# GpSimd's weight splits in feed-forward blocks go to VectorE, and modulation products get windows of steps

## The chip, the core and the metric

One core of a Trainium2 chip runs the whole program. Its engines are TensorE (PE, with PEld for its weight loads), VectorE (DVE), ScalarE (ACT), GpSimd (POOL) and SyncE (SP, whose queue issues most transfers). The metric is device time in microseconds: the median of several runs. Beside it stands one execution that the hardware profiler recorded; durations are read from that one.

## The reference

Two transformer blocks for 256 tokens of width 1024, in fp32. The parts run one after the other, each on what the one before has left in `x`:

```python
x = x + mamba2_mixer(x, ...)                 # first block, layer 0
x = x + conv_ffn(x, ...)                     # ffn0
x = x + diff_attention(x, ...)               # layer 1
x = x + conv_ffn(x, ...)                     # ffn1
mod = silu(c) @ w_ada + b_ada                # 6 x 1024, needed by the second block only
sh1, sc1, ga1, sh2, sc2, ga2 = split(mod, 6)
x = x + ga1 * mixer(rms_norm(x, g_mix) * (1 + sc1) + sh1)   # dsa: attention and a recurrence
x = x + ga2 * conv_ffn_2(rms_norm(x, g_ffn) * (1 + sc2) + sh2)   # ffn2
return rms_norm(x, g_final)

def conv_ffn(x, ln_g, up_w, conv_w, conv_b, down_w):
    u = causal_dwconv(rms_norm(x, ln_g) @ up_w, conv_w, conv_b)   # 1024 -> 2 x 2816, 3 taps over time
    gate, up = u[..., :2816], u[..., 2816:]
    return (silu(gate) * up) @ down_w                             # 2816 -> 1024
```

## The kernel before

**Weights.** All weights come as 360 pieces of up to 128 x 1024, in the order in which they are used, two to a raw chunk of up to 1 MB. SP's queue fetches chunks into four `raw` buffers. A piece is *split*: ACT rounds it to `wh` (L253) and the rest `wl = raw - wh` is computed on DVE (L257) or on POOL (L255). TensorE then takes three products per block of 128 rows, `wh` with the rounded activations `xh`, `wh` with their rest `xl`, and `wl` with `xh` (L379 to L381): 24 matmuls for a full piece. Five `wh` and five `wl` buffers let the splits run ahead; `LEADS` says how far in the first steps of a block.

**Steps.** One piece is one step. `step` runs what was put off to this step, up to two splits, the modulation work, and background work. `POOLED` names the steps of a part, counted from its start, whose splits go to POOL: 1, 3, 5, 7, 9 and 11 in the three feed-forward blocks, so 18 splits, and nine in mamba. The Tile framework then sets the order on each engine; the rows of instruction order below are from its result.

**A feed-forward block.** An up stage has 44 tiles of one piece. The first four (`NRAW`) multiply `rw`, which is `x` before its norm, and are scaled afterwards by `rsb`, the norm's factor (`ru`, L412). The norm's eight parts follow: `ny` on DVE (L493), `xh` on ACT, `xl` on DVE (L469; L498 in the blocks with modulation). From the fifth tile on PE multiplies `xh` and `xl`. Each tile passes a convolution over time (`cv`: one ACT operation, two of L818 on DVE), and each pair of tiles a product (`cv`, L828) and a split into `hh` and `hl`. A down stage has eight tiles of three pieces (8, 8 and 6 row blocks); each ends in an addition to `x` (L509), a square (`sq`, L440, on ACT), a sum of the squares on POOL (L444), and new `rw` (L397) for the next block. When the last `sq` is summed the next block's norm starts.

**Modulation.** `mod` is computed beside all this on DVE, in 96 *units* (`ada`): a transfer of 256 KB on SP's queue into one of two `ada` buffers, then one multiplication with an accumulated sum (L553), and after every second unit a small addition (`mod`, L557). `self.after(i, self.pace)` keeps each unit behind the last DVE split. Before, `ada(rate)` was called in each step, with 0.3 units per step in up stages, 1.0 in down stages, and 0.8 in attention.

Of the kernel before, what the change touches and what calls it, by code (L numbers as in the profile page):

```python
# [29 lines left out]
AHEAD = 3  # L30
DEFER = {"mamba": 2, "ffn": 8}
LEADS = {"attn": [4] * 24, "dsa": [3] * 6, "ffn": [4, 3, 3, 2, 2, 2, 2, 3, 3, 3, 4, 4, 4, 4]}
POOLED = {"ffn": (1, 3, 5, 7, 9, 11), "mamba": (1, 3, 5, *range(22, 44, 4))}
QK_LAG, O_LAG = 3, 3
ADA_AT = 8
ADA_RATE = (0.3, 1.0, 0.8)
ADA_ORDER = list(range(8, 16)) + list(range(8)) + list(range(16, 48))
ATTN_ORDER = [("k", 0), ("q", 0), ("k", 1), ("q", 1), ("v", 0), ("v", 1), ("k", 2), ("q", 2),
              ("k", 3), ("q", 3), ("v", 2), ("v", 3)]
# [136 lines left out]
class Net:  # L176
# [3 lines left out]
    def __init__(self, ctx, tc, a, phases, dbg=None):  # L180
        self.tc, self.nc, self.a, self.dbg = tc, tc.nc, a, dbg or {}
        self.phases = phases
        nc = tc.nc
        self.pieces, self.chunks = _plan(phases)
        self.where = {}
        for j, c in enumerate(self.chunks):
            for i, off in c["p"]:
                self.where[i] = (j, off)
        P = lambda n, b, **k: ctx.enter_context(tc.tile_pool(name=n, bufs=b, **k))
        self.cp = P("const", 1)  # L190
        self.rawp = P("raw", self.RB)
        self.whp = P("wh", self.NS)
        self.wlp = P("wl", self.NS)
        self.xp = P("xn", 1)
        self.tp = P("tmp", 2)
        self.mm = P("mm", 3, space=PSUM)
        self.axp = P("ax", 5, space=PSUM)
        self.dr = P("dr", 1, space=DRAM)
        self.par = self.cp.tile([128, NPAR], F32, name="par")
        self.con = self.cp.tile([128, NCON], F32, name="con")  # L200
        self.x = self.cp.tile([128, 8, T], F32, name="x")
        self.half = self.cp.tile([128, 8], F32, name="half")
        nc.vector.memset(self.half, -0.5)
        self.tuse, self.tname = [], None
        self.since, self.part_of = 0, None
        self.pre = None
        self.onec = self.cp.tile([128, 1], F32, name="onec")
        nc.vector.memset(self.onec, 1.0)
        e = _PC["kv_ln_g"][0]
        nc.scalar.dma_start(self.par[:, 0:e], a["par"][:, 0:e])  # L210
        xv = a["xT"].rearrange("p (k t) -> p k t", k=8)
        for h in range(4):
            nc.sync.dma_start(self.x[:, 2 * h:2 * h + 2, :], xv[:, 2 * h:2 * h + 2, :])
        self.ident = self.con[:, C_ID:C_ID + 128]
        self.ones = self.onec
        self.raw, self.spl = {}, {}
        self.ns, self.nu = 0, 0
        self.bg = deque()
        self.q = []
        self.sched = {}  # L220
        self.adaq, self.rate = None, 0
        self.now = 0
        for j in range(min(self.RB, len(self.chunks))):
            self.load_chunk(j)
            if j == 0:
                nc.sync.dma_start(self.con[:, 0:C_OH], a["con"][:, 0:C_OH])
        self.raws = []
# [75 lines left out]
    def step(self, bg=1):  # L303
        self.q, q = [], self.q
        for n, fn in q:
            if n <= 1:
                fn()
            else:
                self.q.append([n - 1, fn])
        for fn in self.sched.pop(self.now, ()):  # L310
            fn()
        self.now += 1
        self.since += 1
        lead = LEADS.get(self.part_of, ())
        lead = lead[self.since - 1] if self.since <= len(lead) else self.NS
        for _ in range(2):
            if self.ns < self.nu + lead:
                self.split(self.since in POOLED.get(self.part_of, ()))
        if self.adaq:
            self.ada(self.rate)  # L320
        for _ in range(bg):
            if self.bg:
                self.bg.popleft()()
# [44 lines left out]
    def P(self, n, i=0, w=1):  # L368
        o, _ = _PC[n]
        return self.par[:, o + i:o + i + w]  # L370
# [145 lines left out]
    def start_dsa(self):  # L516
        nc, P = self.nc, self.P

        la = self.la = self.cp.tile([128, 4, 8], F32, name="la")
        lam = P("lru_lambda_2", 0, 8)  # L520
        nc.scalar.activation(la[:, 0], lam, AF.Abs)
        self.act(la[:, 0], la[:, 0], AF.Exp, scale=-1.0)
        nc.vector.tensor_scalar(la[:, 1], la[:, 0], 1.0, None, op0=ALU.add)
        self.act(la[:, 2], la[:, 1], AF.Ln)
        nc.vector.scalar_tensor_tensor(la[:, 0], la[:, 1], 1.0, la[:, 0], op0=ALU.subtract, op1=ALU.subtract)
        nc.vector.tensor_scalar(la[:, 3], lam, -1.0, 0.0, op0=ALU.mult, op1=ALU.max)
        nc.vector.tensor_tensor(la[:, 3], la[:, 3], la[:, 2], op=ALU.add)
        nc.vector.tensor_tensor(la[:, 3], la[:, 3], la[:, 0], op=ALU.subtract)
        nc.vector.tensor_scalar(la[:, 1], la[:, 3], -8.0, None, op0=ALU.mult)


    def ada_start(self, pool):
# [266 lines left out]
    def ffn(self, pool, up, down, gs, cw, cb, gate_first, nxt, shift=None, scale=None):  # L799
        nc, P = self.nc, self.P  # L800
        rw = self.rw
        self.table("silu_and_others")
        self.rate = ADA_RATE[0]
        self.since, self.part_of = 0, "ffn"
        xh, xl = self.norm(gs, shift=shift)
        hh = pool.tile([128, NF, T], F32R, name="hh", bufs=1)
        hl = pool.tile([128, NF, T], F32R, name="hl", bufs=1)
        cv = {}

        def conv(j, half):  # L810
            ct = j + NF * half

            def post(pt):
                w = lambda k: P(cw, k * 44 + ct)
                c = pool.tile([128, T], F32, name=f"cv{half}", bufs=3)
                nc.scalar.activation(c, pt, AF.Identity, scale=w(2), bias=P(cb, ct))  # L816
                for d in (1, 2):
                    nc.vector.scalar_tensor_tensor(c[:, d:], pt[:, :T - d], w(2 - d), c[:, d:],  # L818
                                                   op0=ALU.mult, op1=ALU.add)
                cv[j, half] = c  # L820
                if half == 1:
                    self.later(1, lambda: comb(j))
            return post

        def comb(j):
            g, u = (cv.pop((j, 0)), cv.pop((j, 1))) if gate_first else (cv.pop((j, 1)), cv.pop((j, 0)))
            self.act(g, g, AF.Silu)
            nc.vector.tensor_tensor(u, g, u, op=ALU.mult)  # L828
            self.later(1, lambda: self.split_act(u, hh[:, j, :], hl[:, j, :]))

        for j in range(NF):
            for half in range(2):
                if 2 * j + half < NRAW:
                    self.tileR(up, rw, shift is not None, conv(j, half))
                else:
                    self.tileB(up, 8, xh, xl, conv(j, half))
        self.flush()
        self.rate = ADA_RATE[1]
        nxt()
        for m in range(8):  # L840
            self.tileB(down, NF, hh, hl, lambda pt, m=m: self.add_x(m, pt, scale and scale(m)))
        self.flush()
# [39 lines left out]
    def attn(self, pool, nxt):  # L882
        nc, P, ident = self.nc, self.P, self.ident
        tl = lambda n, s, b=1, d=F32: pool.tile(s, d, name=n, bufs=b)
        self.table("exp_and_others")
        self.rate = ADA_RATE[2]
        self.since, self.part_of = 0, "attn"
        scr, units = self.scr1
        self.drain()
# [158 lines left out]
        self.flush()  # L1048
        self.rest()
        nxt()  # L1050
        for m in range(8):
            self.tileB("attn_out_w", 8, oh, ol, lambda pt, m=m: self.add_x(m, pt))
        self.flush()
# [507 lines left out]
```

## Time and profile before

| | us |
|---|---|
| median of 3 runs | 1180.02 (1178.07 to 1181.65) |
| the profiled execution | 1182.38 |
| its span | 1180.6, mean granted clock of TensorE 0.977 |
| PE busy | 1124.2 |
| DVE, ACT, POOL busy | 961.2, 712.3, 221.3 |

The parts follow each other at about 235 us (ffn0), 430 (attention), 557 (ffn1), 761 (dsa) and 974 (ffn2). In a view of groups a row has the line, the engine, the operation, out <- in with their shapes and the count; then the busy time and the mean ns of one; then the engine's idle time just before and what ended it. In a view by stretch each row has the stretch, its length, and for PE, PEld, DVE, ACT and POOL the busy time with the count of instructions. A row of waits says who waited for whom: us in total, times, longest. A timeline row has the start, the duration, the engine and the instruction; in brackets the idle time before it and what ended that.

### The profile page before, as it was taken

To read this page: it belongs to the slowest core of one execution; us is meant where nothing else is said; L and a number is where in the kernel's file an instruction comes from. 1 tells how busy PE (TensorE), PEld (TensorE's weight loads), DVE (VectorE), ACT (ScalarE), POOL (GpSimd) and SP (SyncE) were. 2 spreads that over 40 slices of the span, in tenths; PEclk is the share of its full clock that TensorE was granted. 3 is DMA by queue.
4 is the path that set the end of the run, shared out by engine and by line. 5 is a ranking of instruction groups with operands and counts; after the bars stand their busy time and mean duration, and the time that the engine had idled before them with its cause. 6 is when DMAs were issued, how large, how long until landed. Compare 5 with 4: busy or idle time off the path is not lost.

```text
span 1180.6 us, 23536 instructions
## 1 busy us (share of the span) xinstructions
PE 1124.2 (95%) x9174; PEld 1093.4 (93%) x9174; DVE 961.2 (81%) x1866; ACT 712.3 (60%) x1322; POOL 221.3 (19%) x180
## 2 busy tenths in 40 slices
PE   6899898999999999999899999899999998999997
PEld 5799887989999999988899999899999998999997
DVE  5887998789898878787899998768967888888752
ACT  6567655566666546877466664465587656666541
POOL 3202665242100114222320001100100023200010
PEclk8899989999999999999799999999999999999999
DMA  8455442647756886663456668754452653554530
GB/s 304 140 179 193 152 161 72 219 166 252 266 201 223 275 288 221 190 224 131 168 198 206 207 215 286 250 194 149 170 170 88 223 197 124 205 189 175 172 137 36
DMA packets 50190, 224.80 MB, mean 190 GB/s; under 512 B 5744, under 2 KB 10496, under 8 KB 31136
## 3 DMA queue, kind: packets, MB, share of 16 engines
q1 hardware_dynamic: 41616, 211.53, 52.1%
q10 hardware_dynamic: 7056, 7.46, 2.1%
q0 software_dynamic: 1408, 4.32, 1.2%
q8 instruction: 72, 1.18, 0.4%
q14 instruction: 38, 0.31, 0.1%
HBM read 222.11 MB, written 4.25 MB: 192 GB/s over the span
## 4 chain that ended last, share of the span: by engine, by line
PE 51%; DVE 17%; issue 7%; DMA 7%; ACT 4%; POOL 1%; ACTq 0%; POOLq 0%; DVEq 0%
PE mm L379 15%; PE mm L380 14%; PE mm L381 14%; DMA ada<-in_wada_dram 7%; DVE wl L257 4%; DVE ada L553 2%; DVE cv L818 2%; ACT wh L253 1%; DVE ny L493 1%; PE mm L790 1%; DVE M L705 1%; PE mm L791 1%; PE mm L789 1%; PE mm L921 1%; PE mm L922 1%
## 5 line engine op out<-in xcount | busy, mean ns | idle before, releaser
L253 ACT ACTIVATE wh<-raw 128x1024 fp32r<-128x1024 f32 (+2 forms) x360 | 369.7, 1030 | 264.9 <-PE mm L380 230.4
L257 DVE TENSOR_TENSOR wl<-raw,wh 128x1024 fp32r<-128x1024 f32 (+1 forms) x333 | 397.9, 1195 | 99.5 <-ACT wh L253 96.7
L379 PE MATMUL mm<-xh,wh 128*128 128x256 f32 x1624 | 465.3, 287 | 8.8 <-DVE cv L818 3.4
L380 PE MATMUL mm<-xl,wh 128*128 128x256 f32 x1624 | 460.6, 284 | 6.3 <-DVE xl L469 6.3
L381 PE MATMUL mm<-xh,wl 128*128 128x256 f32 x1624 | 459.8, 283 | 0.0
L379 PEld LDWEIGHTS mm<-xh,wh 128*128 128x128 f32 x1624 | 308.0, 190 | 15.8 <-issue 6.8
L380 PEld LDWEIGHTS mm<-xl,wh 128*128 128x128 f32 x1624 | 308.0, 190 | 8.2 <-DVE xl L469 7.8
L381 PEld LDWEIGHTS mm<-xh,wl 128*128 128x128 f32 x1624 | 308.0, 190 | 0.3 <-DVE xc L1219 0.3
L444 POOL TENSOR_TENSOR sqacc<-sqacc,sq 128x256 f32<-128x256 f32 x42 | 49.6, 1180 | 558.9 <-ACT sq L440 557.3
L379 PE MATMUL mm<-hh,wh 128*128 128x256 f32 x528 | 147.7, 280 | 0.0
L380 PE MATMUL mm<-hl,wh 128*128 128x256 f32 x528 | 147.5, 279 | 0.0
L381 PE MATMUL mm<-hh,wl 128*128 128x256 f32 x528 | 147.2, 279 | 0.0
L818 DVE SCALAR_TENSOR_TENSOR cv<-mm,par,cv 128x255 f32<-128x255 f32 x240 | 114.2, 477 | 4.4 <-ACT cv L816 2.8
L380 PEld LDWEIGHTS mm<-hl,wh 128*128 128x128 f32 x528 | 99.2, 188 | 0.0
L381 PEld LDWEIGHTS mm<-hh,wl 128*128 128x128 f32 x528 | 99.2, 188 | 0.0
L379 PEld LDWEIGHTS mm<-hh,wh 128*128 128x128 f32 x528 | 99.2, 188 | 0.0
L255 POOL TENSOR_TENSOR wl<-raw,wh 128x1024 fp32r<-128x1024 f32 x27 | 71.9, 2662 | 131.5 <-ACT wh L253 126.3
L553 DVE SCALAR_TENSOR_TENSOR ada<-ada,silu_c 128x512 f32<-128x512 f32 x96 | 71.2, 744 | 20.9 <-DMA ada<-in_wada_dram 20.9
L816 ACT ACTIVATE cv<-mm,par 128x256 f32<-128x256 f32 x120 | 65.6, 547 | 0.0
L379 PE MATMUL mm<-rw,wh 128*128 128x256 f32 (+2 forms) x168 | 51.5, 308 | 10.0 <-ACT wh L253 8.9
L380 PE MATMUL mm<-rw,wh 128*128 128x256 f32 (+2 forms) x168 | 52.5, 312 | 0.0
L381 PE MATMUL mm<-rw,wl 128*128 128x256 f32 (+2 forms) x168 | 51.5, 306 | 0.0
(305 smaller groups left out, 1925.4 us busy)
## 6 DMA issues: line engine op xcount, KB each, us to landing
raw<-in_w_dram SPq DMA_DIRECT2D x148, 1024.0 KB, 4.9
ada<-in_wada_dram SPq DMA_DIRECT2D x96, 256.0 KB, 3.7
raw<-in_w_dram SPq DMA_DIRECT2D x23, 896.0 KB, 4.6
raw<-in_w_dram SPq DMA_DIRECT2D x6, 768.0 KB, 4.4
abc<-acs_scr ACTq DMA_DIRECT2D x16, 256.0 KB, 3.3
rel_bias_scr<-rel_bias_row POOLq DMA_DIRECT2D x8, 384.0 KB, 7.0
bias<-rel_bias_scr ACTq DMA_DIRECT2D x16, 128.0 KB, 2.7
x<-in_xT_dram SPq DMA_DIRECT2D x4, 256.0 KB, 4.5
```

What stands on the lines that cost most here:

```text
L253: nc.scalar.activation(wh[:, :n], src, AF.Copy)
L255: nc.gpsimd.tensor_tensor(wl[:, :n], src, wh[:, :n].bitcast(F32), op=ALU.subtract)
L257: self.pace = nc.vector.tensor_tensor(wl[:, :n], src, wh[:, :n].bitcast(F32), op=ALU.subtract)
L379: nc.tensor.matmul(out, h, xh[:, k, :], start=first and a == 0, stop=False)
L380: nc.tensor.matmul(out, h, xl[:, k, :], start=False, stop=False)
L381: nc.tensor.matmul(out, l, xh[:, k, :], start=False, stop=last and a == n - 1)
L444: nc.gpsimd.tensor_tensor(self.acc, self.acc, s, op=ALU.add)
L493: nc.vector.scalar_tensor_tensor(y, self.x[:, k, :], g(k), self.rsb, op0=ALU.mult, op1=ALU.mult)
L553: i = nc.vector.scalar_tensor_tensor(t, t, 1.0, self.sc[:, h * 512:h * 512 + 512], op0=ALU.mult, op1=ALU.mult, accum_out=self.part[:, h, m ...
L705: nc.vector.tensor_tensor(mv[:, h, 0:3:2], e[:, h, 0:3:2, :], CB[:, t // 4, 0:3:2, :], op=ALU.mult)
L816: nc.scalar.activation(c, pt, AF.Identity, scale=w(2), bias=P(cb, ct))
L818: nc.vector.scalar_tensor_tensor(c[:, d:], pt[:, :T - d], w(2 - d), c[:, d:], op0=ALU.mult, op1=ALU.add)
```

## The change

The key "ffn" leaves `POOLED`, so that all splits of the feed-forward blocks are computed on DVE. The rates of modulation units are replaced by windows: within a stage, `ADA_UNITS` gives the first step, the step behind the last, and how many units are spread over them. The output stage of attention gets a window of its own.

```diff
--- before.py
+++ after.py
@@ -30,10 +30,10 @@
 AHEAD = 3
 DEFER = {"mamba": 2, "ffn": 8}
 LEADS = {"attn": [4] * 24, "dsa": [3] * 6, "ffn": [4, 3, 3, 2, 2, 2, 2, 3, 3, 3, 4, 4, 4, 4]}
-POOLED = {"ffn": (1, 3, 5, 7, 9, 11), "mamba": (1, 3, 5, *range(22, 44, 4))}
+POOLED = {"mamba": (1, 3, 5, *range(22, 44, 4))}
 QK_LAG, O_LAG = 3, 3
 ADA_AT = 8
-ADA_RATE = (0.3, 1.0, 0.8)
+ADA_UNITS = {"up": (20, 44, 9), "down": (1, 19, 30), "attn": (5, 22, 16), "attn_out": (1, 6, 6)}
 ADA_ORDER = list(range(8, 16)) + list(range(8)) + list(range(16, 48))
 ATTN_ORDER = [("k", 0), ("q", 0), ("k", 1), ("q", 1), ("v", 0), ("v", 1), ("k", 2), ("q", 2),
               ("k", 3), ("q", 3), ("v", 2), ("v", 3)]
@@ -218,7 +218,7 @@
         self.bg = deque()
         self.q = []
         self.sched = {}
-        self.adaq, self.rate = None, 0
+        self.adaq, self.rate = None, None
         self.now = 0
         for j in range(min(self.RB, len(self.chunks))):
             self.load_chunk(j)
@@ -316,8 +316,10 @@
         for _ in range(2):
             if self.ns < self.nu + lead:
                 self.split(self.since in POOLED.get(self.part_of, ()))
-        if self.adaq:
-            self.ada(self.rate)
+        if self.adaq and self.rate is not None:
+            a, b, n = ADA_UNITS[self.rate]
+            if a <= self.now - self.rate_at < b:
+                self.ada(n / (b - a))
         for _ in range(bg):
             if self.bg:
                 self.bg.popleft()()
@@ -527,6 +529,9 @@
         nc.vector.tensor_tensor(la[:, 3], la[:, 3], la[:, 2], op=ALU.add)
         nc.vector.tensor_tensor(la[:, 3], la[:, 3], la[:, 0], op=ALU.subtract)
         nc.vector.tensor_scalar(la[:, 1], la[:, 3], -8.0, None, op0=ALU.mult)
+
+    def ada_in(self, stage):
+        self.rate, self.rate_at = stage, self.now
 
 
     def ada_start(self, pool):
@@ -800,7 +805,7 @@
         nc, P = self.nc, self.P
         rw = self.rw
         self.table("silu_and_others")
-        self.rate = ADA_RATE[0]
+        self.ada_in("up")
         self.since, self.part_of = 0, "ffn"
         xh, xl = self.norm(gs, shift=shift)
         hh = pool.tile([128, NF, T], F32R, name="hh", bufs=1)
@@ -835,7 +840,7 @@
                 else:
                     self.tileB(up, 8, xh, xl, conv(j, half))
         self.flush()
-        self.rate = ADA_RATE[1]
+        self.ada_in("down")
         nxt()
         for m in range(8):
             self.tileB(down, NF, hh, hl, lambda pt, m=m: self.add_x(m, pt, scale and scale(m)))
@@ -883,7 +888,7 @@
         nc, P, ident = self.nc, self.P, self.ident
         tl = lambda n, s, b=1, d=F32: pool.tile(s, d, name=n, bufs=b)
         self.table("exp_and_others")
-        self.rate = ADA_RATE[2]
+        self.ada_in("attn")
         self.since, self.part_of = 0, "attn"
         scr, units = self.scr1
         self.drain()
@@ -1048,6 +1053,7 @@
         self.flush()
         self.rest()
         nxt()
+        self.ada_in("attn_out")
         for m in range(8):
             self.tileB("attn_out_w", 8, oh, ol, lambda pt, m=m: self.add_x(m, pt))
         self.flush()
```

Lines of the changed file stand 2 to 5 lower (L412 is L414, L493 is L495, L553 is L558). On POOL at the start of ffn1 before (`sqacc` sums the squares of `x`, `rs` is the norm's factor, `oss` belongs to attention):

```order
L297 TENSOR_TENSOR oss<-oss,half 128x2 x4
L444 TENSOR_TENSOR sqacc<-sqacc,sq 128x256 x6
L297 TENSOR_TENSOR rs<-rs,half 128x2
L255 TENSOR_TENSOR wl<-raw,wh 128x1024 x6
L444 TENSOR_TENSOR sqacc<-sqacc,sq 128x256 x6
```

And after the change, at the same place:

```order
L297 TENSOR_TENSOR oss<-oss,half 128x2 x4
L446 TENSOR_TENSOR sqacc<-sqacc,sq 128x256 x6
L297 TENSOR_TENSOR rs<-rs,half 128x2
L446 TENSOR_TENSOR sqacc<-sqacc,sq 128x256 x6
L297 TENSOR_TENSOR rs<-rs,half 128x2
```

The row with the six splits is gone; the sums of squares of the block's end follow the factor directly.

On DVE at the start of ffn1, from the last additions to `x` in attention's output stage to the first parts of the norm, before:

```order
L509 TENSOR_TENSOR x<-mm,x 128x256
L257 TENSOR_TENSOR wl<-raw,wh 128x1024
L397 SCALAR_TENSOR_TENSOR rw<-x,par,rw 128x256
L296 TENSOR_SCALAR rs<-ax 128x2
L553 SCALAR_TENSOR_TENSOR ada,mod_parts<-ada,silu_c 128x512
L557 SCALAR_TENSOR_TENSOR mod<-mod_parts,par 128x1
L553 SCALAR_TENSOR_TENSOR ada,mod_parts<-ada,silu_c 128x512
L412 TENSOR_TENSOR ru<-mm,rsb 128x256
L493 SCALAR_TENSOR_TENSOR ny<-x,par,rsb 128x256 x2
L412 TENSOR_TENSOR ru<-mm,rsb 128x256
L818 SCALAR_TENSOR_TENSOR cv_7065<-ru,par,cv_7065 128x255
```

And after the change, from the factor `rs` on:

```order
L296 TENSOR_SCALAR rs<-ax 128x2
L257 TENSOR_TENSOR wl<-raw,wh 128x1024
L414 TENSOR_TENSOR ru<-mm,rsb 128x256
L495 SCALAR_TENSOR_TENSOR ny<-x,par,rsb 128x256 x2
L823 SCALAR_TENSOR_TENSOR cv_7065<-ru,par,cv_7065 128x255
L471 TENSOR_TENSOR xl_7022<-ny,xh_7021 128x256
L823 SCALAR_TENSOR_TENSOR cv_7065<-ru,par,cv_7065 128x254
L471 TENSOR_TENSOR xl_7022<-ny,xh_7021 128x256
L495 SCALAR_TENSOR_TENSOR ny<-x,par,rsb 128x256 x2
```

The two units and their addition are gone from between `rs` and the first `ru`; a split stands there in their place. The next split comes behind all eight `ny` and `xl`.

On DVE in ffn0's down stage (`rw` and the `xl` behind it are the next block's inputs, of L397), from one tile's addition to `x` to the next, before:

```order
L509 TENSOR_TENSOR x<-mm,x 128x256
L557 SCALAR_TENSOR_TENSOR mod<-mod_parts,par 128x1
L257 TENSOR_TENSOR wl<-raw,wh 128x1024
L397 SCALAR_TENSOR_TENSOR rw<-x,par,rw 128x256
L397 SCALAR_TENSOR_TENSOR xl_4542<-x,par,xh_4541 128x256
L553 SCALAR_TENSOR_TENSOR ada,mod_parts<-ada,silu_c 128x512
L257 TENSOR_TENSOR wl<-raw,wh 128x768
L553 SCALAR_TENSOR_TENSOR ada,mod_parts<-ada,silu_c 128x512
L557 SCALAR_TENSOR_TENSOR mod<-mod_parts,par 128x1
L257 TENSOR_TENSOR wl<-raw,wh 128x1024
L553 SCALAR_TENSOR_TENSOR ada,mod_parts<-ada,silu_c 128x512
L509 TENSOR_TENSOR x<-mm,x 128x256
```

And after the change, at the same tiles:

```order
L511 TENSOR_TENSOR x<-mm,x 128x256
L562 SCALAR_TENSOR_TENSOR mod<-mod_parts,par 128x1
L257 TENSOR_TENSOR wl<-raw,wh 128x1024
L399 SCALAR_TENSOR_TENSOR rw<-x,par,rw 128x256
L399 SCALAR_TENSOR_TENSOR xl_4538<-x,par,xh_4537 128x256
L257 TENSOR_TENSOR wl<-raw,wh 128x768
L558 SCALAR_TENSOR_TENSOR ada,mod_parts<-ada,silu_c 128x512 x2
L257 TENSOR_TENSOR wl<-raw,wh 128x1024
L562 SCALAR_TENSOR_TENSOR mod<-mod_parts,par 128x1
L511 TENSOR_TENSOR x<-mm,x 128x256
```

Units that stood one behind each split now stand in pairs behind every second split. Ahead of the last `x` of this stage there are 23 units in both orders.

## Rows read from the trace of the kernel before

**Rows 1.** Profile page, section 1: busy us, share of the span, instructions.

```profile
PE 1124.2 (95%) x9174; PEld 1093.4 (93%) x9174; DVE 961.2 (81%) x1866; ACT 712.3 (60%) x1322; POOL 221.3 (19%) x180
```

**Rows 2.** Busy time by stretch, then granted clock, DMA share, GB/s.

```profile
235.00:285.00 50.00, 46.73 (x376) 44.66 (x375) 43.93 (x72) 31.53 (x55) 21.28 (x12) 1.00 0.52 180
367.00:430.00 63.00, 63.00 (x537) 63.00 (x536) 54.02 (x106) 34.51 (x51) 7.13 (x6) 1.00 0.79 271
564.50:570.20 5.70, 5.70 (x28) 5.70 (x28) 3.56 (x7) 2.41 (x4) 3.46 (x2) 0.50 0.81 278
580.40:587.20 6.80, 5.34 (x25) 5.34 (x26) 5.67 (x11) 1.72 (x3) 1.12 (x1) 0.50 0.16 22
565.00:612.00 47.00, 43.33 (x310) 41.76 (x310) 42.11 (x77) 26.97 (x48) 15.63 (x7) 0.87 0.47 162
978.00:1020.00 42.00, 38.24 (x309) 37.12 (x309) 36.47 (x64) 27.77 (x52) 16.57 (x7) 1.00 0.41 149
```

**Rows 3.** Waits of PE (us, times, longest) in 235:285, 557:611 and 978:1020.

```profile
PE mm L379 <- DVE cv L818: 1.8, 2, 1.1
...
PE mm L380 <- DVE xl L469: 2.3, 2, 2.0
...
PE mm L379 <- ACT rc L415: 1.9, 1, 1.9
PE mm L379 <- DVE cv L818: 1.2, 2, 1.0
```

**Rows 4.** Timeline of POOL, DVE and PE in ffn1's norm, 566 to 585 us.

```profile
567.80 2.37 POOL L255 TENSOR_TENSOR wl<-raw,wh 128x1024 fp32r<-128x1024 f32 x1 [2.15 <-ACT wh L253]
570.37 2.40 POOL L255 TENSOR_TENSOR wl<-raw,wh 128x1024 fp32r<-128x1024 f32 x1 [0.19 <-ACT wh L253]
578.93 2.59 POOL L255 TENSOR_TENSOR wl<-raw,wh 128x1024 fp32r<-128x1024 f32 x1 [6.17 <-ACT wh L253]
...
568.15 0.43 DVE L412 TENSOR_TENSOR ru<-mm,rsb 128x256 f32<-128x256 f32 x1 [1.83 <-ACT rsb L484]
568.50 4.55 DVE L493 SCALAR_TENSOR_TENSOR ny<-x,par,rsb 128x256 f32<-128x256 f32 x2
579.23 2.57 DVE L469 TENSOR_TENSOR xl<-ny,xh 128x256 fp32r<-128x256 f32 x1
583.58 0.41 DVE L469 TENSOR_TENSOR xl<-ny,xh 128x256 fp32r<-128x256 f32 x1
...
581.86 0.58 PE L380 MATMUL mm<-xl,wh 128*128 128x256 f32 x1 [2.02 <-DVE xl L469]
```

**Rows 5.** Profile page, section 5: DVE's splits, count, busy, mean ns, idle before.

```profile
L257 DVE TENSOR_TENSOR wl<-raw,wh 128x1024 fp32r<-128x1024 f32 (+1 forms) x333 | 397.9, 1195 | 99.5 <-ACT wh L253 96.7
```

**Rows 6.** Groups of DVE by form in 238:280, 565:606, 978:1017 and 770:785.

```profile
L493 DVE SCALAR_TENSOR_TENSOR ny<-x,par,rsb 128x256 f32<-128x256 f32 x8 | 6.2, 815 | 0.0
L818 DVE SCALAR_TENSOR_TENSOR cv<-ru,par,cv 128x255 f32<-128x255 f32 x4 | 1.9, 470 | 0.0
...
L493 DVE SCALAR_TENSOR_TENSOR ny<-x,par,rsb 128x256 f32<-128x256 f32 x8 | 7.2, 935 | 0.0
L469 DVE TENSOR_TENSOR xl<-ny,xh 128x256 fp32r<-128x256 f32 x8 | 5.4, 685 | 0.0
...
L818 DVE SCALAR_TENSOR_TENSOR cv<-ru,par,cv 128x254 f32<-128x254 f32 x4 | 6.2, 1542 | 0.0
...
L493 DVE SCALAR_TENSOR_TENSOR ny<-x,gmdsa,rsb 128x256 f32<-128x256 f32 x8 | 3.5, 476 | 0.0
```

**Rows 7.** Groups of DVE in 367:430: the modulation units.

```profile
L553 DVE SCALAR_TENSOR_TENSOR ada<-ada,silu_c 128x512 f32<-128x512 f32 x22 | 15.1, 686 | 6.5 <-DMA ada<-in_wada_dram 6.5
```

**Rows 8.** Waits of PE in 620:770, the end of ffn1.

```profile
PE ax L452 <- ACT sq L440: 4.0, 1, 4.0
```

**Rows 9.** Profile page, section 6: DMA issues, count, KB each, median us to landing.

```profile
raw<-in_w_dram SPq DMA_DIRECT2D x148, 1024.0 KB, 4.9
ada<-in_wada_dram SPq DMA_DIRECT2D x96, 256.0 KB, 3.7
```

## The prediction

> **What bounds the kernel now.** I read the page's shares first: TensorE (PE) is busy 95% of the 1180.6 us span [rows 1], so a gain can only come from stretches in which PE waits or runs at half clock. The views by stretch say where those are. In the middle of a down stage (367 to 430 us) PE starts 537 matmuls in 63.0 us, one every 0.1173 us, without a pause: that is the pace of an undisturbed step, 24 matmuls or 2.82 us [rows 2]. The starts of the three blocks do not keep it. At 0.1173 us each, 376 matmuls need 44.1 of the 50 us from 235 on, 310 need 36.4 of the 47 us from 565 on, 309 need 36.2 of the 42 us from 978 on [rows 2]. So 5.9, 10.6 and 5.8 us, 22.3 together, is all that faster starts could give back (a few matmul records may be missing, so it is rather less). In ffn1, 2.4 of them belong to a stretch at half clock (564.5 to 570.2: 28 matmuls in 5.70 us for 3.28) that follows waits at the end of attention; a second half-clock stretch (580.4 to 587.2: 25 matmuls in 6.80 for 2.93) follows a wait inside the norm [rows 2].
>
> The waits of PE at these starts then name DVE: `cv` L818 1.8 us in ffn0, `xl` L469 2.3 us in ffn1, `cv` 1.2 and ACT's `rc` 1.9 in ffn2 [rows 3]. The timeline shows why DVE is late. While GpSimd (POOL) runs a split (L255, 2.37 us from 567.80, another from 570.37), two `ny` that DVE starts at 568.50 take 4.55 us; while POOL runs the one from 578.93, one `xl` takes 2.57 us, and 0.41 us at 583.58 when POOL is quiet [rows 4]. PE waited 2.02 us for just that `xl` [rows 4]. A split on POOL does not run beside DVE here: it stops the DVE operation that meets it until it ends.
>
> **The change, part by part.**
>
> *GpSimd's 18 splits go to DVE.* DVE gains 18 operations like its others, 1.195 us each [rows 5]: 21.5 us, 7.2 per block. It loses the stops. Of the groups in the three windows, against the same operation where POOL is quiet (ny 476 ns, xl 410, cv on ru 470) [rows 4, 6]: ny in ffn0 8 x (815 - 476) = 2.7 us; ny in ffn1 8 x (935 - 476) = 3.7 and xl 8 x (685 - 410) = 2.2; cv on ru in ffn2 4 x (1542 - 470) = 4.3 [rows 6]. These four groups alone give 12.9 us; the bound above is 18 stops of 2.57 - 0.41 = 2.16, 38.9 us. I take the middle, 26: DVE's sum falls by some 4 us, little over 1 per block. That is little. What counts is when: the new order puts one split ahead of `ru`, where DVE waited 1.83 us for `rsb` at 568.15 anyway [rows 4], and the next one behind the eight `ny` and `xl`. The norm therefore runs unstopped; in ffn1 it loses the stops of 4.55 - 2 x 0.476 = 3.6 and of 2.16 us, so its last `xl` ends 5.8 us earlier than 583.99.
>
> Here a rule speaks against the change. The rows say that each split on POOL costs DVE about what it saves it, or more [rows 5, 6]. The Trainium skill, Perfetto Trace Analysis, section "Optimizing Scalar/DVE Operations", says that with a saturated DVE it may pay to hand work to GpSimd, and adds that the two share an SBUF read port, so that it might not help. The first half, taken alone, would put 21.5 us of work back on DVE and make the starts slower; the second half is what the trace shows, with 2.57 us for an `xl` of 0.41. SBUF — State Buffer, section "SBUF: two separate sides", has it as an exclusive lock on which the later operation fully blocks; the trace agrees.
>
> What PE gets back, stage by stage:
> - ffn0: the DVE waits are `cv` 1.8 us and smaller ones [rows 3], out of 5.9 lost. I take -2.5. Bounds: -1.0 (the new splits' own delay eats half) and -5.0.
> - ffn1: 10.6 lost, less the 2.4 us at half clock that are older than the norm, leaves 8.2. The norm ends 5.8 us earlier; the second half-clock stretch goes with the wait before it. But the splits put off behind the norm come in a row with the `cv` work, and I leave 1.7 us for PE waiting on them: -6.5. Bounds: -3.0 (PE still falls to half clock after a shorter wait) and -8.2.
> - ffn2: `cv` 1.2, and `rc` 1.9, which on ACT stands behind work on `ru` that DVE delivered late [rows 3]. I take -2.0; bounds 0 and -5.0.
>
> *No modulation units (ada) in the first 20 steps of the up stages.* Each is a DVE multiplication of 0.69 us [rows 7] and a 256 KB transfer. In the order before two of them stand between `rs` and the first `ru` of ffn1: 1.4 us fewer there, which is inside the -6.5, as it helps the delayed splits to catch up. They go to later steps of the same stage, at no cost: even in a down stage, with a unit per piece, DVE is busy for only 54.0 of 63.0 us and PE does not wait [rows 2].
>
> *Down stages: 30 units in steps 1 to 19.* The order shows no end kept free: a unit per weight piece is placed as before, now in pairs behind every second split, and 23 units stand ahead of the last `x` in ffn0, before and now. What differs is the wait for their data. DVE waited 6.5 us for ada transfers from 367 to 430, between 22 units of 686 ns [rows 7]. Only two ada buffers exist: a unit's buffer is free 0.69 us after it starts, and its next data lands L later, so pairs repeat at best every 0.69 + L. Two pieces of a down stage (8, 8 and 6 row blocks in three) take PE 2 x 22 x 0.1173 = 5.16 us. The page's median for an ada transfer, 3.7 us, gives 4.4, and pairs are hidden; the 4.9 us of a raw transfer [rows 9], taken because a raw chunk is now issued right ahead of a pair, gives 5.6, or 0.43 us too much, 12 times: 5 us of lateness per down stage. PE does not feel it inside the stage (splits run some pieces ahead, and before it paused nowhere [rows 2]); it comes out at the end, where PE waits for `x`, `sq` and the sum: 4.0 us at the end of ffn1 [rows 8]. Between the ends I take 4.3 us (the pair's first transfer is queued behind raw, its second is not): 4.99, still hidden, and add 0.5 us at each of two boundaries for the units that spill past the stage into the next norm: +1.0. Bounds: -2 (fewer waits at the boundary) and +10.
>
> *Attention and its output:* 16 units in 17 steps and 6 in 5 instead of 0.8 a step; the output stage has six ahead of its last `x` in both orders. Nothing.
>
> **Sum.** -2.5 - 6.5 - 2.0 + 1.0 = -10.0 us. The profiled execution took 1182.4 us (span 1180.6), so 1172.4; it lies 2.4 above the median of the runs, 1180.0, so I predict 1170.0. 0.3%, what a measurement can tell from no change, is 3.5 us: faster is below 1176.5, slower above 1183.6. Likeliest case's own range: 1163 to 1175.5.
>
> **Rivals.**
> (a) *DVE cannot swallow the splits.* Splits late behind the norm stall PE as the stops did. DVE is idle for 6.1, 4.9 and 5.5 us in the three windows [rows 2] against 7.2 us more work in each. If the stops were only waiting that DVE had to spare, PE ends 1.1 + 2.3 + 1.7 = 5.1 us later: 1185. If half of my gain survives beside it, 1180. For it: DVE becomes the queue for everything at a start. Against it: PE waited for `xl` just when a stop held it [rows 4]. Chance 0.17.
> (b) *The pairs become the wait; slower than before.* Each overrun o costs 24 o over two down stages. It eats the 11 us of the starts and 3.5 more from o = 0.6 us, that is L = 5.1 us, just above a raw transfer's 4.9 [rows 9]. At L = 5.5, o = 1.0, 24 us: 1169 + 24 = 1193, less what the slack of the wait hides; I say 1184 to 1193. For it: DVE already waits 6.5 us on these transfers. Against it: the two transfers of a pair start 0.7 us apart and the median is 3.7. Chance 0.11.
> (c) *More comes back.* The boundary waits shrink too (4.0 us [rows 8], and what follows it), and the starts give 15 of the 22.3 us: 1159 to 1163. Chance 0.13.
>
> Mine: 0.59. Chances: faster 0.59 + 0.13 + 0.01 of (a) = 0.73; same 0.13, of (a) and of the smaller case of (b); slower 0.14. Leaving out the top of (b), the far end of (a) and the bottom of (c), the range is 1161 to 1180.
>
> **What would show it.** Right: no `ny`, `xl` or `cv` above 0.6 us at the three starts; the last `xl` of ffn1's norm some 5 us nearer to its first `ny`; no half-clock stretch after it; matmuls of the first ten tiles nearer 0.1173 us apart; DVE's ada waits near 6.5 us in ffn0's down stage as before. Wrong: PE waiting for `wl` at the starts (a); DVE's ada waits far above 6.5 us per down stage and PE's wait for `sq` above 4.0 (b).

## The result, and the profile after

The changed kernel took **1167.83 us** (median of 5 runs, 1166.40 to 1170.62), the kernel before 1180.20 beside it: a ratio of **0.9896**, 95% interval 0.9876 to 0.9916. The profiled execution has a span of 1168.8 us, 11.8 less than before.

The page's busy line and its line on ada transfers (KB each, median us to landing):

```profile
PE 1119.3 (96%) x9174; PEld 1090.0 (93%) x9174; DVE 949.9 (81%) x1884; ACT 711.2 (61%) x1322; POOL 171.7 (15%) x162
...
ada<-in_wada_dram SPq DMA_DIRECT2D x96, 256.0 KB, 4.2
```

PE's busy sum fell by 5 us, POOL's by 50. DVE's fell from 961.2 to 949.9 although it makes 18 more splits, 21.5 us; so the rest of its work took some 33 us less. Added up in the trace of before, what each DVE operation beside one of the 18 splits took above its usual time comes to 28 us (I had taken 26 for the stops), so I do not put all of the 33 down to them. An ada transfer now lands after 4.2 us instead of 3.7 [rows 9]; I had worked with 4.3.

The same stretches as in [rows 2], moved to where they now lie (PE, PEld, DVE, ACT, POOL, then clock, DMA share, GB/s):

```profile
234.67:284.67 50.00, 49.54 (x414) 48.77 (x413) 44.72 (x84) 35.15 (x61) 4.10 (x6) 1.00 0.65 228
361.47:424.47 63.00, 63.00 (x542) 63.00 (x541) 54.27 (x107) 34.84 (x52) 6.83 (x6) 1.00 0.79 273
431.00:436.00 5.00, 5.00 (x23) 5.00 (x24) 3.33 (x13) 0.91 (x3) 0.71 (x1) 0.50 0.88 266
562.00:609.00 47.00, 46.51 (x380) 45.59 (x379) 42.72 (x83) 32.54 (x57) 0.60 (x1) 0.99 0.52 177
967.30:1009.30 42.00, 40.21 (x318) 39.51 (x318) 36.98 (x71) 29.00 (x54) 0.71 (x1) 0.96 0.46 165
```

Count the matmuls, not the busy time. In the 50 us of ffn0's start there are 414 instead of 376, in the 47 us of ffn1's start 380 instead of 310, in the 42 us of ffn2's 318 instead of 309. At 0.1173 us each that is 4.5, 8.2 and 1.1 us.

DVE in ffn1's norm (timeline), and its groups from 560 to 600, which answer to [rows 4] and [rows 6]:

```profile
564.77 1.23 DVE L257 TENSOR_TENSOR wl<-raw,wh 128x1024 fp32r<-128x1024 f32 x1 [2.96 <-ACT wh L253]
566.25 0.87 DVE L495 SCALAR_TENSOR_TENSOR ny<-x,par,rsb 128x256 f32<-128x256 f32 x2
574.67 0.42 DVE L471 TENSOR_TENSOR xl<-ny,xh 128x256 fp32r<-128x256 f32 x1
```

```profile
L495 DVE SCALAR_TENSOR_TENSOR ny<-x,par,rsb 128x256 f32<-128x256 f32 x8 | 3.6, 478 | 0.0
L471 DVE TENSOR_TENSOR xl<-ny,xh 128x256 fp32r<-128x256 f32 x8 | 3.3, 420 | 0.0
```

The first split waits for ACT in DVE's idle time. From the first `ny` (566.25) to the end of the last `xl` (574.67 + 0.42) it is 8.8 us; before it was 583.99 - 568.50 = 15.5. `ny` and `xl` are back at 478 and 420 ns, and no `ny`, `xl` or `cv` takes more than 0.49 us at the three starts.

Waits of PE in ffn1's start, in ffn2's start, and at the ends of ffn0 and ffn1 (us, times, longest), which answer to [rows 3] and [rows 8]:

```profile
PE mm L381 <- DVE ru L414: 0.2, 1, 0.2
PE mm L382 <- DVE xl L471: 0.2, 1, 0.2
...
PE mm L381 <- ACT rc L417: 1.1, 1, 1.1
...
PE ax L454 <- ACT sq L442: 3.5, 1, 3.5
...
PE ax L454 <- ACT sq L442: 3.0, 1, 3.0
```

The waits for `cv` are gone and that for `xl` is down to 0.2 us. What is left is `rc` in ffn2, and at the ends of the down stages `sq`.

**Where the 11.8 us came from.** The matmuls of the weight pieces can be counted in both traces, and the start of the n-th compared. At ffn0's first tile the changed kernel is 0.3 us ahead, which I take for chance. It gains 4.6 us in ffn0's first 14 tiles, 0.5 in the down stage, loses 2.3 between there and ffn1's second tile, gains 8.0 from there to ffn1's 13th (1.6 of it before the fifth, the first that uses `xh` and `xl`), loses 0.6 at the boundary to dsa, gains 0.2 in dsa and 1.0 in ffn2's start: with the 0.3, 11.7.

### The profile page after: what moved, and what is told of

Its sections match the earlier page's. It is cut to its first block, busy times and chain, and to the rows that moved or that the text cites. A ratio compares the mean times of both kernels' runs of the same rounds, so it can differ in the third digit from the quotient of the medians.

```text
span 1168.8 us, 23504 instructions
## 1 busy us (share of the span) xinstructions
PE 1119.3 (96%) x9174; PEld 1090.0 (93%) x9174; DVE 949.9 (81%) x1884; ACT 711.2 (61%) x1322; POOL 171.7 (15%) x162
## 5 line engine op out<-in xcount | busy, mean ns | idle before, releaser
L257 DVE TENSOR_TENSOR wl<-raw,wh 128x1024 fp32r<-128x1024 f32 (+1 forms) x351 | 419.7, 1197 | 107.4 <-ACT wh L253 105.1
L558 DVE SCALAR_TENSOR_TENSOR ada<-ada,silu_c 128x512 f32<-128x512 f32 x96 | 66.3, 701 | 20.8 <-DMA ada<-in_wada_dram 20.3
L442 ACT ACTIVATE sq<-x 128x256 f32<-128x256 f32 x49 | 20.0, 410 | 57.8 <-DVE x L511 43.7
```

The costliest lines, as they stand in the source:

```text
L257: self.pace = nc.vector.tensor_tensor(wl[:, :n], src, wh[:, :n].bitcast(F32), op=ALU.subtract)
L442: nc.scalar.activation(s, self.x[:, k, :], AF.Square)
L558: i = nc.vector.scalar_tensor_tensor(t, t, 1.0, self.sc[:, h * 512:h * 512 + 512], op0=ALU.mult, op1=ALU.mult, accum_out=self.part[:, h, m ...
```

## The experiments

My theory: GpSimd's splits stop DVE operations that read two SBUF operands, and PE loses time where it waits for these. Rivals: the gain comes from the modulation units that left the starts, or from the changed order of work on DVE.

The ratio is to the kernel before as it ran beside each row (medians of 1179.6 to 1182.9 us), so rows compare best by their ratios.

| run | us, median | ratio to the kernel before | 95% interval |
|---|---|---|---|
| the change | 1167.83 | 0.9896 | 0.9876 to 0.9916 |
| e1, splits only | 1168.56 | 0.9908 | 0.9893 to 0.9924 |
| e2, windows only | 1184.48 | 1.0045 | 1.0027 to 1.0062 |
| e3, spare difference on GpSimd | 1198.66 | 1.0163 | 1.0141 to 1.0184 |
| e4, spare memset on GpSimd | 1170.58 | 0.9917 | 0.9893 to 0.9940 |
| e5, late splits on GpSimd | 1185.68 | 1.0030 | 1.0008 to 1.0051 |
| e6, first split on GpSimd | 1168.74 | 0.9871 | 0.9840 to 0.9902 |
| e7, 20 units in a down stage | 1159.17 | 0.9802 | 0.9777 to 0.9828 |
| e8, as e7, norm in two steps | 1155.92 | 0.9776 | 0.9756 to 0.9795 |
| e9, 16 units in a down stage | 1157.98 | 0.9815 | 0.9793 to 0.9837 |
| e10, as e9, norm in two steps | 1157.78 | 0.9806 | 0.9780 to 0.9832 |
| e11, as e5, units behind the splits | 1180.90 | 1.0008 | 0.9983 to 1.0032 |

**The two halves apart (e1, e2).** e1 is the kernel before with one line changed, e2 the changed kernel with the old line:

```diff
# e1, in the kernel before
-POOLED = {"ffn": (1, 3, 5, 7, 9, 11), "mamba": (1, 3, 5, *range(22, 44, 4))}
+POOLED = {"mamba": (1, 3, 5, *range(22, 44, 4))}
# e2, in the changed kernel
-POOLED = {"mamba": (1, 3, 5, *range(22, 44, 4))}
+POOLED = {"ffn": (1, 3, 5, 7, 9, 11), "mamba": (1, 3, 5, *range(22, 44, 4))}
```

> The kernel before with one half of the change: the 18 splits go from GpSimd to VectorE, the modulation units stay at their old rates. My theory (the stops of VectorE by GpSimd's splits are what the starts lose): the three starts gain nearly all that they gained with the whole change, 4.6, 8.0 and 1.0 us, less about 2 us in ffn1, where ada units stay in VectorE's queue; the boundaries stay as before; 1168 to 1171 us. Rival (the units kept out of the first 20 steps make the gain): 1177 to 1181 us.

> The other half: the new windows for modulation units, with the 18 splits left on GpSimd. My theory: the stops remain, ffn1's start gains at most 2 us from two units less, and the boundaries lose the 2 us that the whole change lost there; 1178 to 1182 us. Rival: 1168 to 1172 us.

ffn1's start in e1, at the place of 562 to 609 above:

```profile
563.00:610.00 47.00, 46.19 (x376) 44.81 (x375) 45.55 (x94) 32.97 (x56) 0.05 (x1) 1.00 0.59 203
```

ffn1's start in e2, and DVE's groups there:

```profile
566.50:613.50 47.00, 41.16 (x297) 39.18 (x296) 41.19 (x65) 26.80 (x48) 14.72 (x6) 0.89 0.40 141
...
L495 DVE SCALAR_TENSOR_TENSOR ny<-x,par,rsb 128x256 f32<-128x256 f32 x8 | 7.4, 949 | 0.0
L471 DVE TENSOR_TENSOR xl<-ny,xh 128x256 fp32r<-128x256 f32 x8 | 5.4, 685 | 0.0
```

With the splits alone the kernel is as fast as with both halves: 376 matmuls in the stretch, although one unit still stands between `rs` and the first `ru`. With the windows alone it is slower than before, with 297, and `ny` and `xl` are stopped as in [rows 6]. The splits are the gain. The windows are worth nothing beside them that these runs can tell, and cost 0.45% without them, more than the 1178 to 1182 us that I expected. e2's trace has a PE wait of 2.2 us for `cv` and 3.4 us at half clock near 610 us, and another 3.4 us at half clock near 808 us, in dsa, neither of which the kernel before has; it does not show why they fell there, and this cost stays open.

**Is it the stop itself? (e3, e4)** In both, DVE executes the same instructions in the same order as in the changed kernel; only GpSimd gets additional work at the 18 places (in e4 ScalarE too, one column each). The code is shortened; lines behind it stand 3 to 5 lower in these two kernels:

```diff
             self.pace = nc.vector.tensor_tensor(wl[:, :n], src, wh[:, :n].bitcast(F32), op=ALU.subtract)
+            if self.part_of == "ffn" and self.since in (1, 3, 5, 7, 9, 11):
+                # e3
+                nc.gpsimd.tensor_tensor(self.spare[:, :n], src, wh[:, :n].bitcast(F32), op=ALU.subtract)
+                # e4, in its place
+                nc.scalar.activation(self.spare[:, 0:1], wh[:, 0:1].bitcast(F32), AF.Copy)
+                nc.gpsimd.memset(self.spare[:, :n], 0.0)
```

> The changed kernel, and beside each of the 18 splits on VectorE GpSimd computes the same difference once more into a spare tile that nobody reads. VectorE's instructions are the same in the same order. My theory (exclusive stop): ny, xl and cv of 2 to 4.5 us come back at the three starts, VectorE has the splits as well, and the whole gain or more is lost; 1178 to 1190 us. Rival (it was the order of work on VectorE): no more than 1 us from 1168.

> As the run with the spare difference, but GpSimd only writes the spare tile (a memset of 128x1024 that waits for one column written by ScalarE), and reads nothing from SBUF. If the stop comes from GpSimd's reading: no ny, xl or cv above 0.6 us, and 1167 to 1170 us. If any GpSimd instruction on SBUF stops VectorE: stops as long as the memsets, and 1172 us or more.

e3 at ffn1's start: POOL's timeline, DVE's groups, waits of PE:

```profile
576.93 5.98 POOL L260 TENSOR_TENSOR spare<-raw,wh 128x1024 f32<-128x1024 f32 x2 [1.79 <-ACT wh L253]
588.37 3.61 POOL L260 TENSOR_TENSOR spare<-raw,wh 128x1024 f32<-128x1024 f32 x1 [5.46 <-ACT wh L253]
...
L498 DVE SCALAR_TENSOR_TENSOR ny<-x,par,rsb 128x256 f32<-128x256 f32 x8 | 9.6, 1232 | 0.0
L837 DVE TENSOR_TENSOR cv<-cv,cv 128x256 f32<-128x256 f32 x4 | 3.9, 964 | 0.0
...
PE mm L384 <- DVE cv L827: 3.6, 4, 1.5
PE mm L384 <- ACT xh L473: 3.0, 1, 3.0
```

e4 in ffn1's norm, POOL's and DVE's timeline:

```profile
570.01 0.96 POOL L261 MEMSET spare<- 128x1024 f32 x1 [5.20 <-ACT spare L260]
...
570.00 0.41 DVE L475 TENSOR_TENSOR xl<-ny,xh 128x256 fp32r<-128x256 f32 x1
570.33 0.41 DVE L838 TENSOR_TENSOR cv<-cv,cv 128x256 f32<-128x256 f32 x1
```

A result that nobody reads costs 1198.66 - 1167.83 = 30.8 us, 1.7 us for each of the 18, and more than the 1190 that I had as the upper end. `ny` takes 1232 ns on average instead of 478, and POOL's own operations take 3.0 (the mean of two) and 3.6 us instead of some 2.4: each holds up the other. The order on DVE is the same, so the rival of order has fallen. The spare difference also keeps its `raw` and `wh` buffers longer, but no wait in this trace names it. In e4 the memset of 0.96 us from 570.01 on has an `xl` and a `cv` beside it, each with two SBUF inputs, and both take their normal 0.41 us; the time is that of the changed kernel, as far as the intervals tell. (The memset is shorter than the difference, so a stop by it would have been shorter too, but none is seen.) So it is GpSimd's reading of SBUF that stops DVE. SBUF — State Buffer, section "SBUF: two separate sides", of the Trainium skill says just that, that a DVE operation with two SBUF inputs is locked out only by a GpSimd operation that reads SBUF; both runs agree.

**Does a stop cost where PE doesn't wait? (e5, e6, e11)** The changed kernel with some splits on GpSimd again, at other steps:

```diff
-POOLED = {"mamba": (1, 3, 5, *range(22, 44, 4))}
+POOLED = {"ffn": (21, 23, 25, 27, 29, 31), "mamba": (1, 3, 5, *range(22, 44, 4))}   # e5
+POOLED = {"ffn": (3,), "mamba": (1, 3, 5, *range(22, 44, 4))}                        # e6
```

> The changed kernel with six splits per block on GpSimd again, but in steps 21 to 31 of the up stages, where TensorE does not wait. If a stop costs time only where TensorE waits for VectorE: stops are seen in the trace (operations of 2 us or more), VectorE has slack for them, and 1166 to 1170 us. If each stop costs the kernel about its 2.2 us wherever it falls: 18 x (2.2 - 1.2) = 18 us more, 1180 or above.

> The changed kernel with only the first split of each block's start on GpSimd (three in all), the one that ran in VectorE's wait for rsb. If that place hides it: VectorE gains 1.2 us at each start, 1165 to 1168 us. If it still stops ru or the first ny: up to 2 us lost in each block, 1169 to 1174 us.

e5, late in ffn0's up stage, where the changed kernel runs without a pause: POOL, DVE and PE in the timeline, and waits of PE from 315 to 355:

```profile
323.26 2.48 POOL L255 TENSOR_TENSOR wl<-raw,wh 128x1024 fp32r<-128x1024 f32 x1 [5.21 <-ACT wh L253]
...
323.41 2.61 DVE L833 TENSOR_TENSOR cv<-cv,cv 128x256 f32<-128x256 f32 x1
326.55 0.47 DVE L823 SCALAR_TENSOR_TENSOR cv<-mm,par,cv 128x255 f32<-128x255 f32 x1
327.28 0.47 DVE L823 SCALAR_TENSOR_TENSOR cv<-mm,par,cv 128x254 f32<-128x254 f32 x1
...
327.89 0.36 PE L381 MATMUL mm<-xh,wh 128*128 128x256 f32 x1 [1.50 <-DVE cv L823]
...
PE mm L381 <- DVE cv L823: 6.0, 4, 1.7
```

My first theory for these steps fell: there is a cost without any wait of PE there before. DVE's slack is an average, and a stop is a delay. The product `cv` <- `cv`,`cv` (L833) stands ahead of the convolution of the next tile (with a unit between) and takes 2.61 us; the convolution's second part starts at 327.28, and PE's next tile, which needs an accumulator that it reads, starts at 327.89 after a wait of 1.50. By the matmul count e5 loses 9.2 us to the changed kernel in these steps of ffn0 and 8.1 in those of ffn1. In ffn2, however, L833 meets all six splits too, and not a tenth of a microsecond is lost. POOL and DVE in the timeline:

```profile
1054.51 2.39 POOL L255 TENSOR_TENSOR wl<-raw,wh 128x1024 fp32r<-128x1024 f32 x1 [3.30 <-ACT wh L253]
...
1049.08 2.41 DVE L833 TENSOR_TENSOR cv<-cv,cv 128x256 f32<-128x256 f32 x1 [0.87 <-ACT cv L288]
1055.60 1.58 DVE L833 TENSOR_TENSOR cv<-cv,cv 128x256 f32<-128x256 f32 x1 [0.55 <-ACT cv L288]
```

Only the first takes 2.41 us there. The other five take 1.58, as in the last row: DVE comes to L833 1.1 us after the split on POOL began, and loses 1.58 - 0.42 = 1.2 us, no more than the split that it does not make; in ffn0 it is 2.61 - 0.42 = 2.2. ffn2 also has no modulation units, and DVE was idle for 0.87 and 0.55 us just ahead of the stopped operations. So I tried the other blocks with their units out of the way:

```diff
 # e11, in e5
-ADA_UNITS = {"up": (20, 44, 9), "down": (1, 19, 30), "attn": (5, 22, 16), "attn_out": (1, 6, 6)}
+ADA_UNITS = {"up": (33, 44, 9), "down": (1, 19, 30), "attn": (5, 22, 16), "attn_out": (1, 6, 6)}
```

> As the run with late splits on GpSimd (steps 21 to 31), but the up stages' nine units come in steps 33 to 43, behind the splits. In that run the stops cost 9.2 us in ffn0 and 8.1 in ffn1, where units stood in the same steps, and nothing in ffn2, which has no units. If a stop costs only where units have used up VectorE's slack: no wait of TensorE in steps 21 to 31 of any block, and 1166 to 1172 us. If the stops of ffn0 and ffn1 cost for another reason: 1180 to 1187 us again.

The waits of PE from 300 to 350 in e11:

```profile
PE mm L381 <- DVE cv L823: 4.2, 4, 1.1
```

The time falls at the lower end of the second range, but the waits have shrunk. In the traces these steps lose 5.5 us in ffn0 and 5.4 in ffn1 without the units, in four waits of up to 1.1 us instead of up to 1.7; that the units are some of it rests on one trace of each kernel, as the intervals of e5 and e11 overlap. The rest, some 1.3 us for each wait, is lost without them. Why ffn2 is spared is not settled by a run; the shorter stops and the idle time ahead of them would account for it.

In e6 the first split does run where DVE waited, and yet not in that wait alone:

```profile
566.26 2.41 POOL L255 TENSOR_TENSOR wl<-raw,wh 128x1024 fp32r<-128x1024 f32 x1 [1.50 <-ACT wh L253]
...
566.49 0.42 DVE L414 TENSOR_TENSOR ru<-mm,rsb 128x256 f32<-128x256 f32 x1 [2.51 <-ACT rsb L486]
566.83 2.52 DVE L495 SCALAR_TENSOR_TENSOR ny<-x,par,rsb 128x256 f32<-128x256 f32 x2
```

It begins 0.2 us before `ru` and stops the first two `ny`, which take 2.52 us instead of 0.87. `ru`, whose other operand `mm` lies in TensorE's accumulators and not in SBUF, is not stopped (0.42 us). The 1.65 us lost are a little more than the 1.2 that DVE saves by not making the split; the time is that of the changed kernel, as far as the intervals tell.

**The ends of the down stages (e7 to e10).** The prediction read from the order that the ends are not kept free, and PE's waits for `sq` above say that they matter. These runs move units from the down to the up stages:

```diff
-ADA_UNITS = {"up": (20, 44, 9), "down": (1, 19, 30), "attn": (5, 22, 16), "attn_out": (1, 6, 6)}
+ADA_UNITS = {"up": (16, 44, 17), "down": (1, 17, 20), "attn": (5, 22, 16), "attn_out": (1, 6, 6)}   # e7, e8
+ADA_UNITS = {"up": (14, 44, 21), "down": (1, 16, 16), "attn": (5, 22, 16), "attn_out": (1, 6, 6)}   # e9, e10
-DEFER = {"mamba": 2, "ffn": 8}
+DEFER = {"mamba": 2, "ffn": 4}   # e8, e10
```

> The changed kernel with 20 units instead of 30 in a down stage (steps 1 to 16) and 17 instead of 9 in an up stage (steps 16 to 43): the last two tiles of a down stage have no unit. If the units late behind their transfers hold the last x of a stage (it came 5.0 us behind the last matmul at the end of ffn0, 4.6 before): last x within 2 us of the matmuls, PE's waits for sq near 1 us instead of 3.5 and 3.0, less half clock after it; 4 to 8 us less, 1160 to 1164 us. If x waits for something else there: 1166 to 1169 us.

> As the run with 20 units, and the norm's eight parts are put into two steps instead of one (four each). If the burst of eight parts in one step is what still delays the work on ru at the starts (PE waits 1.1 us for rc in ffn2): 1 to 3 us less than that run. If the xl that come later hold PE instead: 1 to 4 us more.

> The changed kernel with 16 units in a down stage (steps 1 to 15) and 21 in an up stage (steps 14 to 43). The last x of a down stage already comes right behind its matmuls with 20 units. If nothing is left to gain there: the same as the run with 20, 1157 to 1162 us. If the units in steps 14 to 19 delay VectorE's cv, which frees TensorE's accumulators, as the late splits on GpSimd did: 2 us or more above that run.

> The same with the norm's parts in two steps of four. Together with the pair of runs with 20 units it tells what the two steps are worth: 1 to 3 us less than the run beside it if the burst of eight parts delays the work on ru; the same within 1 us if the difference of the pair before was chance.

The end of ffn0 in the changed kernel: DVE in the timeline, and the stretch:

```profile
427.38 0.69 DVE L558 SCALAR_TENSOR_TENSOR ada<-ada,silu_c 128x512 f32<-128x512 f32 x1 [1.46 <-DMA ada<-in_wada_dram]
429.98 0.42 DVE L511 TENSOR_TENSOR x<-mm,x 128x256 f32<-128x256 f32 x1
...
425.00:437.00 12.00, 8.49 (x51) 8.28 (x50) 7.86 (x22) 2.93 (x6) 0.71 (x1) 0.72 0.86 284
```

The same in e7, with PE:

```profile
423.88 2.35 DVE L257 TENSOR_TENSOR wl<-raw,wh 128x1024 fp32r<-128x1024 f32 x2
426.15 0.41 DVE L511 TENSOR_TENSOR x<-mm,x 128x256 f32<-128x256 f32 x1
...
425.49 0.50 PE L454 MATMUL ax<-onec,sqacc 128*128 128x1 f32 x4
427.22 0.50 PE L454 MATMUL ax<-onec,sq 128*128 128x1 f32 x4
...
425.00:437.00 12.00, 12.00 (x104) 12.00 (x103) 7.48 (x16) 6.16 (x11) 1.40 (x2) 1.00 0.76 255
```

The last `x` starts at 426.15 behind two splits, with no unit between; in the changed kernel it stood behind a pair that came late, at 429.98. PE does not pause, and makes 104 matmuls from 425 to 437 at full clock; the changed kernel makes 51, with a clock of 0.72. By the matmul count e7 gains 6.8 us on the changed kernel at the end of ffn0 and 6.7 at the end of ffn1. The medians differ by less, 8.7 us: the traced executions lie at opposite ends of their runs (1156.97 and 1170.62). With 16 units instead of 20 nothing more is gained. The norm in two steps looks 0.3% better in one pair of runs and the same in the other: it is worth nothing that these runs can tell. The version to keep is e7: 0.9802 (0.9777 to 0.9828) of the kernel before, which e8 to e10 do not clearly beat.

## Why the prediction was right

The time (1170.0 forecast, 1167.8 measured) and the mechanism were right. The terms were off in both directions, and that they add up so well is in part luck.

- *The stops.* Shown by e1 to e4. They come to 28 us in the trace of before, where I took 26 as the middle of two bounds; the largest group, 7.8 us on the product `cv` (L828), was not among my four. DVE's sum fell by 11.3 us where I had 4. That a split on POOL stops whatever DVE operation meets it was put too broadly: `ru` took its usual 0.43 us beside one in [rows 4].
- *ffn0, -2.5 forecast, -4.6 measured.* Mis-sized: I went by the waits that name DVE (1.8 us and less), and took the missing matmuls (5.9 us) only as a bound. PE was idle for only 3.3 of the 50 us there (50.00 - 46.73 in [rows 2]); the rest of the 5.9 is matmuls that start further apart, mostly the first ones behind a pause, while PE counts as busy. The count was nearer.
- *ffn1, -6.5 forecast, -8.0 measured.* Of the 8.0, 1.6 came ahead of the norm's products: the half-clock stretch there, which I had left out as older than the norm, lasted 3.4 us (from 559.7) instead of 6.8 (from 563.4). That part is luck. The 6.4 from the fifth tile on are what I forecast. The norm became 6.7 us shorter, where I had 5.8; no half clock followed it, and PE's waits there sum to 0.4 us where I had left 1.7 for the delayed splits. That the units moved away help there is not shown: with them in place e1 gains 8.5 us in the same tiles, 5.5 of it from the fifth on, and its time is the same.
- *ffn2, -2.0 forecast, -1.0 measured.* PE still waits 1.1 us for `rc`, on ACT behind a `wh` that itself waits for PE; in this execution a stretch at half clock followed (982.9 to 986.3 us). In e1's execution none did, and the same tiles gain 2.1.
- *Pairs and boundaries, +1.0 forecast, +2.2 measured.* A pair's transfers land after 4.2 us (4.3 assumed), and DVE waits for them 6.2 us in ffn0's down stage, as before [rows 7]:

```profile
L558 DVE SCALAR_TENSOR_TENSOR ada<-ada,silu_c 128x512 f32<-128x512 f32 x22 | 14.9, 689 | 6.4 <-DMA ada<-in_wada_dram 6.2
```

But the loss at the boundary to attention, which I had put down to units that spill past the stage, does not need the pairs: e1, with the old rates, loses 2.8 us in the same place, and the changed kernel 2.3. The half-clock stretch after the boundary lasted 3.4 us in the profiled execution before, 6.8 in that of the changed kernel, 10.2 in e1. It follows PE's pause for `sq`, and varies from one execution to the next: in e4, where DVE's work has the order of the changed kernel, the pause was 1.4 us and no such stretch followed.
- *Rival (a)* had the right fear (more work on DVE), but the stops were real: e3. *Rival (b)* needed transfers of 5.1 us and got 4.2. *Rival (c)* did not come with this change; its time came with e7 (1159.2), which frees the ends.

## What to carry to other kernels

An operation on GpSimd that reads SBUF is not free help for a busy VectorE: each of these took 2.4 us or more to save VectorE 1.2, and held it up for 1.6 on average at the starts. In two of three blocks such splits cost time also far from the stage's start, through the accumulators that VectorE frees. Size the loss of a stage by counting its matmuls against the pace of an undisturbed stage, not by the named waits alone. And look in the instruction order at whether a change does what its numbers say: the windows here kept the ends of the stages as full as before, and freeing them in earnest was worth another 0.7% by the medians, 0.9% by the ratios.

## What the runs showed of the hardware

- A memset of 128x1024 on GpSimd (0.96 us) left VectorE operations with two SBUF inputs beside it at 0.41 us; a difference of the same size stopped them for up to 2.2 us, and was itself slowed, from 2.4 to 3.6 us (e3, e4).
- Beside the same GpSimd split `ru`, with one operand in SBUF and one in TensorE's accumulators, took its usual 0.42 us, while `ny`, with two in SBUF, was stopped (e6).
- In e11 four of the five stops of L833 in ffn0 (2.6 us instead of 0.42) cost PE some 1.3 us each, and as many in ffn1. In ffn2, where five of six were shorter (1.58 us) and DVE was idle just before, they cost nothing.
- A pause of PE of about 3 us (`sq`, 3.5 and 3.0) was followed by stretches of 6.8 us at a granted clock of 0.50, the lower of its two levels, in the changed kernel. With e7 PE does not pause there, and no such stretch follows either boundary.
